# Conv stage: shifted copies by way of DRAM, the last tiles' taps behind all products, a padded sample past

## The chip, the core and the metric

One core of a Trainium2 chip runs the whole program. TensorE (PE) multiplies, VectorE (DVE), ScalarE (ACT) and GpSimd (POOL) work on rows, SyncE (SP) issues the DMAs. The metric is the device time of one execution in microseconds, the median of several runs.

## The reference

One inference step of a trunk of four layers for 512 prompt tokens and 8 sequences of 8 sample tokens, `D` = 1024, all in float32. Layers 0 and 3 have the convolution mixer that the change is about, layer 1 has attention, layer 2 pooling, and each is followed by a feed-forward block with a small convolution. The mixer:

```python
def conformer_conv(h, prefix, w_in, w_dw, ln_g, ln_b, w_out):
    a, g = jnp.split(h @ w_in, 2, axis=-1)
    u = a * jax.nn.sigmoid(g)
    up = jnp.concatenate([prefix.astype(u.dtype), u], axis=1)
    y = depthwise_causal(up, w_dw)
    y = jax.nn.silu(layer_norm(y, ln_g, ln_b))
    return y @ w_out, up[:, -(CONV_WIDTH - 1):]
```

`w_dw` has 31 taps for each of the 1024 channels. `prefix` is zero for the prompt and the last 30 rows for a sample sequence; the last 30 rows of `up` are an output.

## The kernel before

Channels lie on the partitions, tokens along the rows: 512 prompt tokens and 8 x 8 of the samples, in two halves of 288 columns. The mixer works in 8 tiles of 128 channels. For each tile i:

- **Products** (`pc`): 96 matmuls of 288 columns in tiles 2 to 7 (four groups of 24 by `mm6`), 96 by `mm3` in tiles 0 and 1, which `f_consume` runs together while the normed input comes in. A weight tile is loaded by SyncE (`raw`, 1 MB), and ScalarE and VectorE split it into two parts (`w`). The low part on VectorE frees `raw` for the next load.
- **GLU**: ScalarE's sigmoid (`sg`), then VectorE's product into `ub`, one row per channel: 30 zeros, the 512 prompt tokens, and behind them 8 sample windows of 30 past and 8 new tokens. The past comes by DMA from `sconv`.
- **Shifted copies** (`xs`, `shift` at L925): to run 31 taps as matmuls of 128 rows, 32 channels are laid out four times, each time a token further on. For each tile that is 16 copies from SBUF to SBUF of 32 rows x 540 columns (L930), eight for each half `p` of the channels.
- **Taps** (`pts`, `taps` at L938): 8 steps x 4 groups of channels, for each of which a diagonal `dg` (VectorE, `diag`) is multiplied with `xs`; a step covers four taps. They run in two visits of 4 steps each. `take` copies the result to `y` on ScalarE.
- **Sample taps** (`prods`, `tree`): products on GpSimd, sums on GpSimd or VectorE.
- `outs` (L921, L922) writes the state output `uc` in two transfers.

`f_conv_tail` then does the layer norm: a mean from tiles 0 to 5 (`st`), everything centred by it, the squares (`sq`), the exact mean and variance, and the product `pd` with `w_out` behind it (`f_out`). The taps of tile 7 run here, by halves of the tokens (256 columns).

Order: every piece is a task with an engine, a duration and a priority. `Flow.run` takes again and again the task that can start earliest, by priority among equals, so that durations and priorities set the order in which each engine's instructions are written out; on the chip each engine then runs its list in that order. `XQ` is a made-up engine that stands for the time of a transfer, `st` and `sg` count places in the shared buffers that a task takes and gives back. The products with `ada` (`adaps`), which make the scale and shift of the next normalization, are put in between.

SyncE has its own list as well: a DMA that waits holds up those behind it.

Of the kernel before, what the change touches and what calls it, by code (L numbers as in the profile page):

```python
# [30 lines left out]
D = 1024  # L31
KT = 8
NF = 22
# [6 lines left out]
XW = 512 + 4 * TG - 4  # L40

# [149 lines left out]
class Trunk:  # L191
# [681 lines left out]
    def f_conv(self, fl, l, j, dep, wdep, pdep=None):  # L873

        nc, I, O = self.nc, self.I, self.O
# [20 lines left out]
        def up(i):  # L898
            return U[i][:, 0:543]

        def us(i):
            return U[i][:, 543:847].rearrange("p (s t) -> p s t", t=38)

        def pre(i):
            U[i] = self.slot([128, 847], F32, name="ub")
            nc.gpsimd.memset(up(i)[:, 0:30], 0.0)
            nc.gpsimd.memset(up(i)[:, 542:543], 0.0)
            nc.sync.dma_start(out=us(i)[:, :, 0:30], in_=I["sconv"][j, :, i])
# [6 lines left out]
        def glu(i, h):  # L915
            pa = P[i, 0, h]
            nc.vector.tensor_tensor(up(i)[:, 30 + HP * h:30 + HP * h + HP], G[i][:, h, :HP], pa[:, :HP], OP.mult)
            nc.vector.tensor_tensor(us(i)[:, 4 * h:4 * h + 4, 30:38], self.sv(G[i][:, h]), self.sv(pa), OP.mult)

        def outs(i):  # L920
            nc.sync.dma_start(out=O["uc"][j, :, i, 0:30], in_=up(i)[:, 512:542])  # L921
            nc.sync.dma_start(out=O["uc"][j, :, i, 30:270].rearrange("p (s t) -> p s t", t=30), in_=us(i)[:, :, 8:38])  # L922
# [23 lines left out]
        def conv(i, a0, a1):  # L946
            if a0 == 0:
                P[i, "t"] = self.bank("pts")
            taps(P[i, "t"], i, a0, a1, 0, 512)

        def take(i):
            nc.scalar.activation(yv(i)[:, :, :HP], P[i, "t"].rearrange("p (a c) -> p a c", a=2), AF.Copy)

# [26 lines left out]
        val, tap_end, join_end, y = {}, {}, {}, {}  # L980
        for i in range(8):
# [24 lines left out]
            t += [fl.add("POOL", 2.7, lambda a=(i, n): prods(*a), gs, st=1, prio=pr + n) for n in range(2)]  # L1006
            fl.add("FREE", 0.0, lambda: None, t, xs, sg=1)
            t = t[1:]
            for n, d in ((16, 2.4), (8, 1.6), (4, 1.0), (2, 0.7), (1, 0.6)):
                t = fl.add(("POOL", "DVE"), (d, d / 2), lambda e, a=(i, n): tree(*a, e), t, sg=2 if n == 1 else 0,  # L1010
                           prio=pr + 2, bias=(0, 1.0))
            y[i] = [t]
            if i == 7:
                break
            t = None
            for a in range(0, TG, 4):
                t = fl.add("PE", 3.7, lambda a=(i, a, a + 4): conv(*a), t, xs, take=0 if a else 1,
                           sg=2 if a + 4 == TG else 0, prio=pr + 1)
            tap_end[i] = t
            join_end[i] = fl.add("ACT", 0.62, lambda i=i: take(i), t, give=1, prio=pr + 2)  # L1020
            y[i].append(join_end[i])
        self.w_ahead(fl, val[6][1])
        self.cv = dict(yv=yv, y=y, ready=xs, taps=taps, wdep=val[7][1], gate=[val[n][1] for n in range(8)])

    def f_conv_tail(self, fl, l, j, adep=None):

# [6 lines left out]
        q2, o, sb, sq, r, tl = {}, {}, {}, {}, {}, {}  # L1033
# [14 lines left out]
        def tap(h, a):  # L1048
            if a == 0:
                o[h] = self.bank("pts")  # L1050
            cv["taps"](o[h], 7, a, a + 4, HP * h, HP * h + HP)

        def join(h):
            nc.scalar.activation(yv(7)[:, h, :HP], o[h][:, :HP], AF.Copy)
# [51 lines left out]
        for h in range(2):  # L1106
            a = self.f_sum(fl, lambda m, h=h: yv(m)[:, h], stg[h], range(4), lambda m: True, lambda m: m in (2, 3),
                           [ready[m] for m in range(4)], take=1, prio=8000)
            a = self.f_sum(fl, lambda m, h=h: yv(m)[:, h], stg[h], range(4, 6), lambda m: False, lambda m: True, a,
                           [ready[m] for m in range(4, 6)], prio=8000)  # L1110
            a = fl.add("ACT", 0.4, lambda h=h: copy(h, 0, stg[h], "ACT"), a)
            a = self.f_mean(fl, lambda h=h: sb[h, 0], stg[h], a)
            c0.append(fl.add("ACT", 0.4, lambda h=h: nc.scalar.activation(mu(0, h), st[h][:, :H], AF.Copy, scale=8.0 / 6), a))

        last = []
        for h in range(2):
            t = None
            for a in range(0, TG, 4):
                t = fl.add("PE", 2.0, lambda h=h, a=a: tap(h, a), t, cv["ready"], take=0 if a else 1, prio=8003 + h)
            last.append(fl.add("ACT", 0.4, lambda h=h: join(h), t, give=1, prio=-1))  # L1120
        rs = []
        for h in range(2):
            cs, ss = [], []
            for m in range(8):
                if m < 6:
                    c = fl.add("POOL", 0.75, lambda h=h, m=m: centre(h, m, 0, "POOL"), c0[h], prio=8000)
                else:
                    c = fl.add("DVE", 0.36, lambda h=h, m=m: centre(h, m, 0, "DVE"), c0[h], last[h] if m == 7 else None,
                               ready[m], prio=-1)
                cs.append(c)  # L1130
                ss.append(fl.add("ACT", 0.34, lambda h=h, m=m: square(h, m), c, prio=0 if m > 5 else 8000))
                if h == 0 and m == 5:
                    fl.add("ACT", 1.5, lambda: self.table(AF.Sqrt), ss[-1], prio=0)
# [1399 lines left out]
def pack(inp, depth=DEPTH):  # L2533
# [42 lines left out]
    wd = np.concatenate([g["conv_w_dw"], np.zeros((2, 4 * TG - CW, D), f)], 1).reshape(2, TG, 4, 8, 4, 32)  # L2576
    A["wst"] = np.ascontiguousarray(wd.transpose(0, 2, 5, 3, 4, 1)).reshape(2, 128, 8, 4 * TG)

    A["sconv"] = np.ascontiguousarray(g["state_conv"].transpose(0, 3, 1, 2).reshape(2, 8, 128, 8, 30).transpose(0, 2, 1, 3, 4))
# [65 lines left out]
def out_shapes(depth=DEPTH):  # L2645
    return {
        "y": (128, 2, 8, H), "uc": (2, 128, 8, 270), "ff": (4, 128, NF, 18), "pl": (128, 8, 15), "ps": (128, 2, 32, 15),
# [17 lines left out]
def unpack(o):  # L2665
    import numpy as np
    yp, ys = unpack_x(o["y"])
    uc = o["uc"].transpose(0, 2, 1, 3).reshape(2, D, 270)
    p_conv = uc[:, :, :30].transpose(0, 2, 1)[:, None]
    s_conv = uc[:, :, 30:].reshape(2, D, 8, 30).transpose(0, 2, 3, 1)  # L2670
# [36 lines left out]
```

## Time and profile before

| | us |
|---|---|
| median of 3 runs | 2942.83 (2942.69 to 2952.84) |
| the profiled execution | 2944.08 |
| its span | 2942.3 |
| TensorE busy | 2795.8 (95%) |
| mean granted TensorE clock | 0.98 |
| conv stage of layer 0, up to the first `pd` | 58 to 274.05 |
| conv stage of layer 3, up to the first `pd` | 2213 to 2436.73 |

A profile gives, for each instruction, its start, its length, and what ended the idle time of its engine before it. A clock of 0.5 is 1.2 GHz, 1.0 is 2.4 GHz. DMA shares are of all 16 DMA engines together.

### The profile page before, as it was taken

To read this page: it belongs to the slowest core of one execution; us is meant where nothing else is said; L and a number is where in the kernel's file an instruction comes from. 1 tells how busy PE (TensorE), PEld (TensorE's weight loads), DVE (VectorE), ACT (ScalarE), POOL (GpSimd) and SP (SyncE) were. 2 spreads that over 40 slices of the span, in tenths; PEclk is the share of its full clock that TensorE was granted. 3 is DMA by queue.
4 is the path that set the end of the run, shared out by engine and by line. 5 is a ranking of instruction groups with operands and counts; after the bars stand their busy time and mean duration, and the time that the engine had idled before them with its cause. 6 is when DMAs were issued, how large, how long until landed. Compare 5 with 4: busy or idle time off the path is not lost.

```text
span 2942.3 us, 50575 instructions
## 1 busy us (share of the span) xinstructions
PE 2795.8 (95%) x20437; PEld 2473.9 (84%) x20437; DVE 1581.6 (54%) x3411; ACT 982.3 (33%) x2103; POOL 508.7 (17%) x936
## 2 busy tenths in 40 slices
PE   7898999999999999989999979999998989999998
PEld 5565799999989656889999958999997647999997
DVE  5235554454554576464455686455556336655555
ACT  3114332222355565332222244222223125422223
POOL 3234100000144234010000061000003342100001
PEclk9999999999999999999999989999999999999999
DMA  8536133334344355323322279222233453222221
GB/s 292 131 98 210 72 140 125 151 136 152 122 155 148 119 165 210 131 79 140 112 78 81 100 187 149 72 89 84 87 100 110 99 141 131 87 81 92 78 82 64
DMA packets 137705, 358.94 MB, mean 122 GB/s; under 512 B 66336, under 2 KB 72384, under 8 KB 116224
## 3 DMA queue, kind: packets, MB, share of 16 engines
q1 hardware_dynamic: 134656, 347.31, 36.8%
q0 software_dynamic: 2816, 8.39, 0.8%
q8 instruction: 162, 2.65, 0.4%
q14 instruction: 71, 0.58, 0.1%
HBM read 319.37 MB, written 18.39 MB: 115 GB/s over the span
## 4 chain that ended last, share of the span: by engine, by line
PE 79%; DMA 7%; DVE 7%; SPq 3%; issue 2%; ACT 1%; POOL 1%; DVEq 0%; ACTq 0%; POOLq 0%
PE pa L355 6%; PE pa L358 6%; PE pa L356 6%; PE pb L355 5%; PE pb L356 5%; PE pb L358 5%; PE pd L355 5%; PE pd L358 5%; PE pd L356 5%; PE pts L942 3%; PE pd L347 2%; SPq L930 2%; PE pd L348 2%; PE pd L349 2%; PE adaps L419 2%
## 5 line engine op out<-in xcount | busy, mean ns | idle before, releaser
L274 DVE TENSOR_TENSOR w<-raw,w 128x2048 fp32r<-128x2048 f32 (+1 forms) x117 | 259.4, 2217 | 388.0 <-ACT w L273 388.0
L355 PE MATMUL pa<-h,w 128*128 128x288 f32 x1280 | 363.0, 298 | 5.6 <-ACT w L273 5.6
L356 PE MATMUL pa<-h,w 128*128 128x288 f32 x1280 | 360.0, 296 | 0.0
L355 PE MATMUL pb<-h,w 128*128 128x288 f32 x1216 | 341.1, 295 | 0.0
L356 PE MATMUL pb<-h,w 128*128 128x288 f32 x1216 | 340.9, 295 | 0.0
L355 PE MATMUL pd<-u,w 128*128 128x288 f32 x1152 | 323.8, 296 | 0.0
L356 PE MATMUL pd<-u,w 128*128 128x288 f32 x1152 | 322.9, 295 | 0.0
L738 POOL COPY so<-ab 128x2 f32<-128x2 f32 x88 | 17.0, 193 | 1520.5 <-ACT ab L708 1520.5
L273 ACT ACTIVATE w<-raw 128x2048 fp32r<-128x2048 f32 (+1 forms) x117 | 218.8, 1870 | 176.2 <-PE pd L358 176.2
L358 PE MATMUL pa<-h,w 128*128 128x288 f32 x1280 | 275.2, 296 | 1.0 <-DVE w L274 1.0
L355 PEld LDWEIGHTS pa<-h,w 128*128 128x128 f32 x1280 | 242.0, 189 | 24.3 <-issue 17.6
L358 PE MATMUL pb<-h,w 128*128 128x288 f32 x1216 | 260.1, 295 | 0.0
L358 PE MATMUL pd<-u,w 128*128 128x288 f32 x1152 | 246.4, 295 | 0.0
L356 PEld LDWEIGHTS pa<-h,w 128*128 128x128 f32 x1280 | 241.9, 189 | 0.0
L355 PEld LDWEIGHTS pb<-h,w 128*128 128x128 f32 x1216 | 228.7, 188 | 0.0
L356 PEld LDWEIGHTS pb<-h,w 128*128 128x128 f32 x1216 | 228.6, 188 | 0.0
L355 PEld LDWEIGHTS pd<-u,w 128*128 128x128 f32 x1152 | 216.7, 188 | 6.7 <-issue 6.7
L303 DVE TENSOR_TENSOR w<-raw,w 128x512 fp32r<-128x512 f32 x213 | 171.5, 848 | 90.2 <-ACT w L298 89.7
L356 PEld LDWEIGHTS pd<-u,w 128*128 128x128 f32 x1152 | 216.6, 188 | 0.0
L496 DVE TENSOR_TENSOR rtmp<-pd,mod 128x32 f32<-128x32 f32 x368 | 68.6, 186 | 263.3 <-PE pd L358 174.2
L358 PEld LDWEIGHTS pa<-h,w 128*128 128x128 f32 x1280 | 206.6, 189 | 1.5 <-DVE w L274 1.5
L718 ACT ACTIVATE ab<-ab 128x576 f32<-128x576 f32 x88 | 60.4, 687 | 435.5 <-DVE ab L737 435.5
(356 smaller groups left out, 6520.5 us busy)
## 6 DMA issues: line engine op xcount, KB each, us to landing
raw<-in_w_dram SPq DMA_DIRECT2D x165, 1024.0 KB
ada<-in_ada_dram SPq DMA_DIRECT2D x192, 512.0 KB
xs<-ub SPq DMA_DIRECT2D x256, 67.5 KB
raw<-in_w_dram SPq DMA_DIRECT2D x16, 768.0 KB
x<-in_x_dram SPq DMA_DIRECT2D x8, 576.0 KB
xsp<-x SPq DMA_DIRECT2D x8, 576.0 KB
x<-xsp SPq DMA_DIRECT2D x8, 576.0 KB
out_wo_dram<-in_sw_dram SPq DMA_DIRECT2D x8, 512.0 KB
```

The lines of the kernel that those rows point to most:

```text
L273: nc.scalar.activation(w[:, 0, :width], r[:, :width], AF.Copy)
L274: self.lo_eng.tensor_tensor(w[:, 1, :width], r[:, :width], w[:, 0, :width], OP.subtract)
L303: self.eng(eng).tensor_tensor(w[:, 1, sl], r[:, sl], w[:, 0, sl], OP.subtract)
L347: nc.tensor.matmul(ps[:, :H], hi, mv(k, 0, h), start=first, stop=False)
L348: nc.tensor.matmul(ps[:, :H], hi, mv(k, 1, h), start=False, stop=False)
L349: nc.tensor.matmul(ps[:, :H], lo, mv(k, 0, h), start=False, stop=last)
L355: nc.tensor.matmul(ps[h][:, :H], hi, mv(k, 0, h), start=first, stop=False)
L356: nc.tensor.matmul(ps[h][:, :H], hi, mv(k, 1, h), start=False, stop=False)
L358: nc.tensor.matmul(ps[h][:, :H], lo, mv(k, 0, h), start=False, stop=last)
L496: nc.vector.tensor_tensor(t, self.sv(ps), self.bc(G, m, h), OP.mult)
L718: self.nc.scalar.activation(acc, acc, AF.Silu)
L942: nc.tensor.matmul(o[32 * g:32 * g + 32, :c1 - c0], DG[i][:, g * TG + a], X[i, g // 2][:, g % 2, 4 * a + c0:4 * a + c1], start=(a == 0), s ...
```

## The change

1. **Copies by way of DRAM.** `ub`'s prompt part is stored to a DRAM tensor `ub` (one transfer, 128 rows of 543), and the shifted copies are loaded from there, four transfers a tile (two for each half of the channels), each with all four shifts in the pattern of its source: 4 x 32 x 540, to 128 partitions. The zeros now are 31 in front, and the weights `wst` are padded in front instead of behind.
2. **State and past.** `sconv` comes padded to 38 columns a window, so it is one run of 304 per row; `uc` is written as one run of 334 per row, and the host takes the 30 that count.
3. **Taps.** Tiles 0 to 4: all 8 steps in one visit. Tiles 5 to 7: by halves of the tokens, behind all products (`late`), in the order 5, 6, 7 for the first half, then the second. VectorE subtracts the mean as it takes them out of PSUM (`take`, `take_s` in the tail). `diag` may run three tiles ahead.
4. **Mean.** The first mean is of tiles 0 to 3 (scale 2.0 for 8/6).
5. **Sample taps of tile 7** are on VectorE, by halves of the sequences (`prods_h`, `tree_h`).

```diff
-                for k in range(4):
-                    c = 64 * p + 32 * g
-                    nc.sync.dma_start(out=x[32 * k:32 * k + 32, g], in_=U[i][c:c + 32, k:k + XW])
+                u = I["ub"][j, i, 64 * p + 32 * g:64 * p + 32 * g + 32]
+                nc.sync.dma_start(out=x[:, g], in_=bass.AP(tensor=u.tensor, offset=u.offset, ap=[[1, 4], [UP, 32], [1, XW]]))
...
-        def conv(i, a0, a1):
-            if a0 == 0:
+        def conv(i, c0, c1):
+            if c0 == 0:
                 P[i, "t"] = self.bank("pts")
-            taps(P[i, "t"], i, a0, a1, 0, 512)
+            taps(P[i, "t"][:, c0:c1], i, 0, TG, c0, c1)
...
-            t = [fl.add("DMA", 0.7, lambda i=i: outs(i), gs, prio=pr)]
+            t = fl.add("DMA", 0.5, lambda i=i: store(i), gs, prio=pr - 1000)
+            kept = [fl.add("DMA", 0.6, lambda i=i: outs(i), gs, prio=pr), t]
+            t = fl.add("XQ", 2.5, lambda: None, t)
             xs = []
             for p in range(2):
-                x = fl.add("DMA", 2.7, lambda a=(i, p): shift(*a), gs, st=1, prio=pr - 1000)
-                xs.append(fl.add("XQ", 2.5, lambda: None, x))
-            xs.append(fl.add("DVE", 1.15, lambda i=i: diag(i), t_wr, tap_end.get(i - 2), prio=pr - 500))
...
+                x = fl.add("DMA", 1.0, lambda a=(i, p): shift(*a), t, st=1, prio=pr - 1000)
+                xs.append(fl.add("XQ", 3.5, lambda: None, x))
+            kept += xs
+            xs.append(fl.add("DVE", 1.15, lambda i=i: diag(i), t_wr, tap_end.get(i - 3), prio=pr - 500))
...
+                for h in range(2):
+                    t = fl.add("DVE", 1.15, lambda h=h: prods_h(h), gs[h], st=1, prio=-1)
+                    kept.append(t)
+                    for n, d in ((16, 0.6), (8, 0.35), (4, 0.25), (2, 0.2), (1, 0.18)):
+                        t = fl.add("DVE", d, lambda a=(h, n): tree_h(*a), t, sg=1 if n == 1 else 0, prio=-1)
+                    y[i].append(t)
...
+            if i < 5:
+                tap_end[i] = fl.add("PE", 7.3, lambda i=i: conv(i, 0, 512), xs, take=1, sg=2, prio=pr + 1)
...
+        for h in range(2):
+            for i in range(5, 8):
+                tap_end[i, h] = fl.add("PE", 3.75, lambda a=(i, HP * h, HP * h + HP): conv(*a), late[i], val[7][1],
+                                       tap_end.get((i - 1, h)), tap_end.get((i, 0)) if h else None,
+                                       take=0 if h else 1, sg=2 if h else 0, prio=7900 + 10 * h)
...
+        def take(h, m):
+
+            nc.vector.tensor_tensor(yv(m)[:, h, :HP], cv["bank"](m)[:, HP * h:HP * h + HP], mu(0, h)[:, :HP], OP.subtract)
...
+                    c = [fl.add("DVE", 0.4, lambda h=h, m=m: take(h, m), c0[h], cv["tap_end"][m, h], give=h, prio=-1),
+                         fl.add("DVE", 0.18, lambda h=h, m=m: take_s(h, m), c0[h], ready[m][h], prio=0)]
...
+    wd = np.concatenate([np.zeros((2, 4 * TG - CW, D), f), g["conv_w_dw"]], 1).reshape(2, TG, 4, 8, 4, 32)
...
+        I["ub"] = tc.nc.dram_tensor("ub", (2, 8, 128, UP), F32, kind="Internal").ap()
```

The DMA list of SyncE at tile 3 of layer 0, in the kernel before (`raw` is a weight load for a later tile, the last row belongs to tile 4):

```order
L930 DMA xs_1195<-ub_772 32x540 x8
L2491 DMA raw_1210<-in_w_dram 128x2048
L930 DMA xs_1238<-ub_772 32x540 x8
L921 DMA out_uc_dram<-ub_772 128x30
L922 DMA out_uc_dram<-ub_772 128x8x30
L930 DMA xs_1312<-ub_1072 32x540 x8
```

And in the changed kernel:

```order
L926 DMA ub<-ub_783 128x543
L923 DMA out_uc_dram<-ub_783 128x334
L2513 DMA raw_1171<-in_w_dram 128x2048
L933 DMA xs_1201<-ub 128x1x540 x2
L933 DMA xs_1204<-ub 128x1x540 x2
L926 DMA ub<-ub_1074 128x543
```

The sixteen copies with the weight load in their middle have become a store in front and four loads (two rows of two) behind the weight load.

SyncE at tile 7 of layer 0, before (`ada` are loads for the products that are put in between):

```order
L389 DMA ada_1835<-in_ada_dram 128x1024
L389 DMA ada_1837<-in_ada_dram 128x1024
L2491 DMA raw_1861<-in_w_dram 128x2048
L930 DMA xs_1873<-ub_1543 32x540 x8
L930 DMA xs_1905<-ub_1543 32x540 x8
L921 DMA out_uc_dram<-ub_1543 128x30
```

And changed, from the store of tile 7 on:

```order
L926 DMA ub<-ub_1447 128x543
L923 DMA out_uc_dram<-ub_1447 128x334
L2513 DMA raw_1835<-in_w_dram 128x2048
L391 DMA ada_1875<-in_ada_dram 128x1024
L391 DMA ada_1877<-in_ada_dram 128x1024
L933 DMA xs_1887<-ub 128x1x540 x2
L933 DMA xs_1895<-ub 128x1x540 x2
```

The loads of tile 7 now stand behind a weight load and two `ada` loads, where its copies stood behind the weight load alone.

TensorE in the tail of layer 0, before: the taps of tile 7 (`pts_1950` and `pts_1976`, one for each half of the tokens) with the sums for the layer norm between them:

```order
L942 MATMUL pts_1950<-xs_1873,dg_1665 32x256 x2
L942 MATMUL pts_1950<-xs_1905,dg_1665 32x256 x2
L540 MATMUL st_1817<-y_713,ones_85 32x288 x2
L540 MATMUL st_1817<-y_1014,ones_85 32x288 x2
L540 MATMUL sq_2027<-sq_1974,ones_85 32x288 x4
L540 MATMUL st_1770<-y_1409,ones_85 32x288 x2
L540 MATMUL st_1770<-y_1882,ones_85 32x288 x2
L540 MATMUL sq_1933<-sq_1938,ones_85 32x288 x4
L942 MATMUL pts_1976<-xs_1873,dg_1665 32x256 x2
```

And changed, where the second half of tile 7 (`pts_1976` again, by chance) begins:

```order
L945 MATMUL pts_1976<-xs_1887,dg_1445 32x256 x2
L945 MATMUL pts_1976<-xs_1895,dg_1445 32x256 x2
L421 MATMUL adaps_1933<-ada_1812,cm_92 32x512 x2
L421 MATMUL adaps_1933<-ada_1814,cm_92 32x512 x2
L542 MATMUL st_1450<-y_1353,ones_85 32x288 x2
L542 MATMUL st_1450<-y_1764,ones_85 32x288 x2
L542 MATMUL sq_1633<-sq_1617,ones_85 32x288 x4
L945 MATMUL pts_1976<-xs_1887,dg_1445 32x256 x2
```

The late taps of tiles 5 and 6 are all in front of this place now, an `ada` pair stands between the halves of tile 7, and behind its first half the sums of the first half of the tokens.

In the list of products the taps have moved back, too. Counted in single product matmuls from the first one on, those of layer 0 stand behind 246 (tile 0), 360 (2 and 1), 552 (3) and 576 (4), those of layer 3 behind 288 (0 and 1), 480 (2), 504 (3) and 624 (4), and the others behind all 768.

## Rows read from the trace of the kernel before

**Rows 1.** The page: the span, and TensorE's busy time with its share and instructions.

```profile
span 2942.3 us, 50575 instructions
...
PE 2795.8 (95%) x20437; PEld 2473.9 (84%) x20437; DVE 1581.6 (54%) x3411; ACT 982.3 (33%) x2103; POOL 508.7 (17%) x936
```

**Rows 2.** Sums by stretch: window, length, busy PE PEld DVE ACT POOL, clock, DMA share, GB/s.

```profile
58.00:274.05 216.05, 187.46 (x1416) 119.95 (x1414) 75.09 (x101) 43.60 (x91) 74.29 (x68) 0.95 0.55 150
...
2213.00:2436.73 223.73, 198.08 (x1488) 133.44 (x1486) 96.69 (x149) 53.81 (x115) 83.45 (x79) 0.95 0.48 130
```

**Rows 3.** Groups of TensorE, layer 0: busy, mean ns, idle before, what ended it.

```profile
L942 PE MATMUL pts<-xs,dg 128*32 128x512 f32 x448 | 68.9, 647 | 19.1 <-DMA xs<-ub 19.1
...
L942 PE MATMUL pts<-xs,dg 128*32 128x256 f32 x128 | 11.3, 433 | 6.4 <-DMA xs<-ub 6.4
L419 PE MATMUL adaps<-ada,cm 128*32 128x512 f32 x80 | 10.4, 597 | 0.0
```

**Rows 4.** The same view, conv stage of layer 3.

```profile
L942 PE MATMUL pts<-xs,dg 128*32 128x512 f32 x448 | 64.4, 612 | 12.2 <-DMA xs<-ub 12.0
...
L942 PE MATMUL pts<-xs,dg 128*32 128x256 f32 x128 | 10.8, 425 | 6.0 <-DMA xs<-ub 6.0
```

**Rows 5.** Sums by stretch, two of those at half clock (columns as in Rows 2).

```profile
75.20:78.60 3.40, 3.40 (x15) 0.91 (x19) 0.00 (x0) 0.00 (x0) 0.72 (x1) 0.50 0.74 101
...
2413.30:2420.10 6.80, 3.24 (x26) 1.41 (x27) 0.00 (x0) 0.00 (x0) 0.00 (x0) 0.50 0.70 158
```

**Rows 6.** Timeline of TensorE, layer 3: start, length, instruction, [idle before <-what ended it].

```profile
2277.71 0.40 PE L355 MATMUL pc<-h,w 128*128 128x288 f32 x1
...
2281.08 3.64 PE L942 MATMUL pts<-xs,dg 128*32 128x512 f32 x32
...
2295.72 4.49 PE L942 MATMUL pts<-xs,dg 128*32 128x512 f32 x28 [3.47 <-DMA xs<-ub]
...
2416.78 4.10 PE L942 MATMUL pts<-xs,dg 128*32 128x256 f32 x28 [5.47 <-DMA xs<-ub]
```

**Rows 7.** Timeline of VectorE, SyncE (SPq) and GpSimd in the same tile.

```profile
2281.99 4.48 DVE L303 TENSOR_TENSOR w<-raw,w 128x512 fp32r<-128x512 f32 x4
2282.04 5.91 SPq L930 DMA_DIRECT2D xs<-ub  x8
2282.22 2.49 POOL L961 TENSOR_TENSOR prod<-ub,par 128x960 f32<-128x960 f32 x1 [16.30 <-DVE ub L918]
...
2288.05 0.53 SPq L2491 DMA_DIRECT2D raw<-in_w_dram  x1
```

**Rows 8.** Timeline of SyncE: a weight load alone, and a store of x alone.

```profile
730.22 0.33 SPq L2491 DMA_DIRECT2D raw<-in_w_dram  x1
...
794.31 0.33 SPq L488 DMA_DIRECT2D xsp<-x  x1
```

**Rows 9.** DMA from 729.2 to 737.2, 40 slices of 0.2 us (busy tenths), packets.

```profile
DMA  4000000009903968799799595220000000000000
...
DMA packets 145, 1.07 MB, mean 133 GB/s; under 512 B 16, under 2 KB 16, under 8 KB 16
```

**Rows 10.** DMA from 794 to 799, slices of 0.125 us; queue: packets, MB, share of 16.

```profile
DMA  0000000009889998997930000000000600000000
...
q1 hardware_dynamic: 144, 0.59, 28.6%
```

**Rows 11.** DMA from 62.4 to 66.4: shifted copies alone.

```profile
DMA packets 193, 0.29 MB, mean 73 GB/s; under 512 B 64, under 2 KB 64, under 8 KB 192
...
q1 hardware_dynamic: 192, 0.28, 29.9%
```

**Rows 12.** DMA from 976.9 to 987.9: transfers of eight rows.

```profile
q1 hardware_dynamic: 224, 0.03, 1.6%
...
cvg<-cvt SPq DMA_DIRECT2D x16, 2.0 KB
```

**Rows 13.** Groups of TensorE behind the conv stage of layer 0 (columns as in Rows 3).

```profile
L419 PE MATMUL adaps<-ada,cm 128*32 128x512 f32 x52 | 8.7, 649 | 2.5 <-DMA ada<-in_ada_dram 2.5
```

More of the change, by code (lines that the diff above doesn't have):

```diff
@@ L898, in up @@
         def up(i):
-            return U[i][:, 0:543]
+            return U[i][:, 0:UP]
         def us(i):
-            return U[i][:, 543:847].rearrange("p (s t) -> p s t", t=38)
+            return U[i][:, UP:].rearrange("p (s t) -> p s t", t=38)
         def pre(i):
[L905 to L908, printed above, removed]
+            U[i] = self.slot([128, UP + 304], F32, name="ub")
+            nc.gpsimd.memset(up(i)[:, 0:31], 0.0)
+            nc.sync.dma_start(out=U[i][:, UP:], in_=I["sconv"][j, :, i])
         def sig(i, h):
@@ L916, in glu, with store @@
             pa = P[i, 0, h]
-            nc.vector.tensor_tensor(up(i)[:, 30 + HP * h:30 + HP * h + HP], G[i][:, h, :HP], pa[:, :HP], OP.mult)
+            nc.vector.tensor_tensor(up(i)[:, 31 + HP * h:31 + HP * h + HP], G[i][:, h, :HP], pa[:, :HP], OP.mult)
             nc.vector.tensor_tensor(us(i)[:, 4 * h:4 * h + 4, 30:38], self.sv(G[i][:, h]), self.sv(pa), OP.mult)
         def outs(i):
-            nc.sync.dma_start(out=O["uc"][j, :, i, 0:30], in_=up(i)[:, 512:542])
-            nc.sync.dma_start(out=O["uc"][j, :, i, 30:270].rearrange("p (s t) -> p s t", t=30), in_=us(i)[:, :, 8:38])
+            nc.sync.dma_start(out=O["uc"][j, :, i], in_=U[i][:, UP - 30:])
+        def store(i):
+            nc.sync.dma_start(out=I["ub"][j, i], in_=up(i))
         def shift(i, p):
@@ L979, in product @@
                 self.mm6([P[i, c, h] for h in range(2)], w(), k * 256 + c * 128, mv, k, k == 0, k == KT - 1)
-        val, tap_end, join_end, y = {}, {}, {}, {}
+        val, tap_end, join_end, y, late = {}, {}, {}, {}, {}
         for i in range(8):
@@ L1012, in f_conv @@
[L1012 to L1021, printed above, removed]
+                x = fl.add("DMA", 1.0, lambda a=(i, p): shift(*a), t, st=1, prio=pr - 1000)
@@ new lines, in f_conv @@
+                xs.append(fl.add("XQ", 3.5, lambda: None, x))
+            kept += xs
+            xs.append(fl.add("DVE", 1.15, lambda i=i: diag(i), t_wr, tap_end.get(i - 3), prio=pr - 500))
+            if i < 7:
+                t = [fl.add("POOL", 2.7, lambda a=(i, n): prods(*a), gs, st=1, prio=pr + n) for n in range(2)]
+                kept += t
+                for n, d in ((16, 2.4), (8, 1.6), (4, 1.0), (2, 0.7), (1, 0.6)):
+                    t = fl.add(("POOL", "DVE"), (d, d / 2), lambda e, a=(i, n): tree(*a, e), t, sg=2 if n == 1 else 0,
+                               prio=pr + 2, bias=(0, 1.0))
+                y[i] = [t, t]
+            else:
+                y[i] = []
+                for h in range(2):
[4 more added lines that the diff above has]
+                    y[i].append(t)
@@ new lines, in f_conv @@
+            fl.add("FREE", 0.0, lambda: None, kept, sg=1)
+            if i < 5:
+                tap_end[i] = fl.add("PE", 7.3, lambda i=i: conv(i, 0, 512), xs, take=1, sg=2, prio=pr + 1)
+                join_end[i] = fl.add("ACT", 0.62, lambda i=i: take(i), tap_end[i], give=1, prio=pr + 2)
+                y[i].append(join_end[i])
+            else:
+                late[i] = xs
+        for h in range(2):
[3 more added lines that the diff above has]
+                                       take=0 if h else 1, sg=2 if h else 0, prio=7900 + 10 * h)
@@ L1022, in f_conv @@
         self.w_ahead(fl, val[6][1])
-        self.cv = dict(yv=yv, y=y, ready=xs, taps=taps, wdep=val[7][1], gate=[val[n][1] for n in range(8)])
+        self.cv = dict(yv=yv, y=y, bank=lambda i: P[i, "t"], tap_end=tap_end, wdep=val[7][1], gate=[val[n][1] for n in range(8)])
     def f_conv_tail(self, fl, l, j, adep=None):
@@ L1106, in f_conv_tail @@
         for h in range(2):
[L1107 to L1110, printed above, removed]
+            a = self.f_sum(fl, lambda m, h=h: yv(m)[:, h], stg[h], range(4), lambda m: True, lambda m: True,
+                           [ready[m] for m in range(4)], take=1, prio=6000)
             a = fl.add("ACT", 0.4, lambda h=h: copy(h, 0, stg[h], "ACT"), a)
             a = self.f_mean(fl, lambda h=h: sb[h, 0], stg[h], a)
[L1113 to L1120, printed above, removed]
+            c0.append(fl.add("ACT", 0.4, lambda h=h: nc.scalar.activation(mu(0, h), st[h][:, :H], AF.Copy, scale=2.0), a))
         rs = []
```

48 lines of the change are left out of this document (25 added, 23 removed).

## The prediction

> **What bounds the kernel now.** I read the page first: TensorE is busy 95% of the span [rows 1], so a stage is worth what TensorE waits in it. Then the sums by stretch for the two conv stages, each up to the first matmul into `pd`: in layer 0 TensorE is busy 187.5 of 216.05 us at a mean clock of 0.95, in layer 3 198.1 of 223.7 [rows 2]: 28.6 and 25.6 us idle. The groups of instructions say what ended the idle time: before the taps it is always the shifted copies, 19.1 + 6.4 us in layer 0 and 12.0 + 6.0 in layer 3 [rows 3, 4], together 43.5 us. Third, the granted clock: eight stretches of 3.4 us (two of them 6.8) run at 0.50, 34 us in all, half of it lost, 17 us [rows 5] (two of the eight). So all that the change can win in the conv stages is about 60 us.
>
> Why the copies are late is seen in one tile of layer 3. Its last group of 24 products runs from 2277.71 to 2281.08 (3.37 us, so 13.5 for a tile), and a half of the taps takes 3.64, a whole 7.28 [rows 6]. The GLU ends at 2282.0. SyncE then issues eight copies (5.91 us), the weight load `raw` at 2288.05, and eight more; the last taps get their copy at 2295.72, 14.6 us after the product ended [rows 6, 7]. Issue time and the weight load in the middle make up that delay.
>
> **The change, part by part.** *Issues.* Sixteen copies of 0.7 to 0.8 us each go; a store, one state output in place of two, and four loads come. SyncE gets some 8 us a tile back, off the path: what counts is when the last load lands.
>
> *Where the loads stand.* In the new order each tile's row is store, output, `raw`, four loads. `raw` waits, as before, for VectorE to finish the low halves of the weights, at 2281.99 + 4.48 = 2286.47, 5.4 us after the product ended [rows 7], and the loads stand behind it. A `raw` alone, issued at 730.22 [rows 8], has its last packets in slice 27 of 0.2 us from 729.2, 4.4 us after issue [rows 9]. So a tile's loads begin 5.4 + 4.4 = 9.8 us after its product. The store is hidden under this: one of 576 KB, issued at 794.31 [rows 8], had its last data packets in slice 21 of 0.125 us from 794, 2.3 us after issue [rows 10], and the new one is of 271 KB, and the GLU before it 1 us.
>
> *How long the loads take.* This the trace of before doesn't show. A load has 128 rows of 2160 bytes, but its source is written as 4 shifts by 32 rows by 540, its destination as 128 partitions. The nearest rows: the copies of 32 rows leave 192 packets for four, 64 of them small: 32 rows and 16 small ones each [rows 11]. The `raw` leaves 128 + 16 [rows 9]. The transfers of eight rows leave 224 for fourteen that landed, all small: 16 each, so eight rows and eight others [rows 12]. I read the extra packets as one completion for each engine used: sixteen, but eight where there are only eight rows. So a transfer seems to be dealt out by its outermost dimension. With four there I take it that the load runs on four engines; were it dealt by the 128 partitions, it would be sixteen. The Trainium skill, page "DMA: Bandwidth & Descriptors", section "Why a DMA increments its semaphore by 16 and not by 1", says the same more sharply: the number of engines is the largest up to 16 that divides the slowest dimension of both sides, which here is four. By that page the four are always the lowest-numbered; no row here shows which they are.
>
> In the sum all loads queue on the same four engines. Were each dealt to a different four, a tile's loads would take as long as on sixteen.
>
> A packet: the 4608-byte rows of the store take 28.6% of 16 engines in 5 us, 22.9 us for 128, 179 ns [rows 10], which by bytes is 84 ns for 2160. The copies of 2160 bytes now take 29.9% of 16 x 4 us, 19.1 us for 128, 149 ns [rows 11]; those are short transfers from SBUF to SBUF, 2 rows an engine. The loads stream, as the store does, so I take 86 ns. Four engines: 32 packets a load, 128 a tile, 11 us (19 at the other end). Sixteen engines: 2.8 us (4.8).
>
> So, after its product, a tile's copies are there at 9.8 + 11 = 21 us on four engines, or, when the engines still have the tile before, 14 us after that one (its `raw` share, 3 us, and 11). On sixteen it is 12.6 us.
>
> *New places of the taps.* The change moves them back, whole tiles at a time, and those of tiles 5 to 7 behind all products. I put the waits together from the order, with 3.37 for 24 products, 7.28 for a tile's taps, 1.04 for an `ada` pair (10.4 us for ten [rows 3]). Layer 3, time 0 at the end of products(1), on four engines: copies(0) at -3.4 + 21 = 17.6, wanted at 13.5: wait 4.1, taps end 24.9. Copies(1) at 31.4: wait 6.5, end 38.7. Products of 2 and 3, interleaved, end at 48.8 and 52.2; copies(2) at 69.8, wanted at 65.7: 4.1. Copies(3) at 83.8, wanted at 80.5: 3.3. Taps(4): products(4) end at 94.5, copies at 115.5, wanted at 109: 6.5. Products 6 and 7 end at 131 and 144.5. Tile 5 waits nothing; tile 6 has its copies at 152, wanted at 149.2: 2.8; tile 7, behind 6 on the same engines, at 166, wanted at 164: 2. Sum 29. Layer 0 in the same way: 4.8 (0), 5.1 (2), 9.2 (1), 4.2 (3), 3.3 (4), 2.6 (6) and 4.4 (7, whose loads stand behind a `raw` that waits for GpSimd and two `ada` loads): 34. Together 63 us of waits in place of 43.5: +19.5. On sixteen engines none of these is left.
>
> *Other edits.* Moving the `ada` loads ahead takes away the 2.5 us wait of layer 0 and the 1.0 of layer 3 [rows 13] (the second is of the same kind): -3.5. The clock: fourteen waits of 2 to 9 us replace some 25 of 0.3 to 5.5 [rows 6] (the longest, and one of the middle); I take the same loss, 17 us, bounds -9 and +9. Whole visits of the taps, rather than halves, spare a few switches: -2, bounds -8 and 0. The tail changes work at equal cost: VectorE centres tiles 5 to 7 straight from PSUM instead of ScalarE copying first, and it does the sample taps of tile 7 under the late taps; if that cover fails, two half tiles of them stand before the last sums; GpSimd now takes 2.5 us for one half of a tile's products [rows 7], so bound +5. The mean over four tiles needs no sums of tiles 4 and 5 and is early. Wider `sconv` and `uc` rows: one run a partition for eight, off the path.
>
> Sum against the profiled 2944.08 us (0.04% over the median 2942.83): +19.5 - 3.5 + 0 - 2 = +14, less 2 for the median and rounding: **2956 us**.
>
> **Rivals.** *Sixteen engines.* For it: all transfers with 128 partitions in this trace leave 16 small packets. Against: none of them has a first dimension of four on one side. Then 43.5 of copies, 3.5 of `ada`, 15 of the 17 of the clock and 2 to 5 of switches go: -64 to -67, and in the tail, at full clock, a few more: 2876 us (2862 to 2892).
>
> *Four engines and slow packets*, the one on the other side: if a packet on the four engines costs the 149 ns of the present copies, a tile's loads take 19 us, and with its `raw` 22 us, more than the 20.8 of a tile's products and taps: then the copies set the pace, at some 8 us more in nine of the fourteen waits, +72: 3028. It decides from about 130 ns a packet. Against it: the store's rate.
>
> *Half effect*: the loads use eight engines or overlap from two ends: 5.5 us a tile, copies at 15.3, nearly all hidden: some 2895.
>
> That the order is not what it says is no rival: the order of the built kernel has the taps where I count them.
>
> **How the numbers follow.** Four engines at the store's rate 0.52, own range 2925 to 2985 (the waits can be wrong by 15, the clock by 9, the tail by 5); sixteen engines 0.36; eight 0.05; slow packets 0.07. The range takes the first two: 2862 to 2985, leaving out the slow packets and the edges. About 0.5% (15 us) is what a measurement can tell, so the bounds lie at 2928 and 2957.5. Faster: 0.35 of the sixteen, 0.05 of the eight, 0.03 of the four: 0.43. Within: 0.26 of the four and 0.01: 0.27. Slower: 0.23 of the four and 0.07: 0.30. The forecast itself stands just under the upper bound.
>
> **What would show it.** The packets of a load: 128 + 4 if four engines, 128 + 16 if sixteen. The stretch of a tile's loads: DMA share at a quarter for 11 us, or full for 3. Taps with one wait a tile of 3 to 9 us, or none. `raw` to the next products: no new wait on `w`. If the idle time before the taps falls under 10 us in both layers and the time doesn't reach 2900, the clock or the tail has taken it, and my sum is wrong there. If the waits are there but under 40 us together, the start of the loads (9.8 us) is what I have too late.

## The result: slower by 1.45%, on the side of the four engines

The changed kernel takes 2988.28 us (median of 4 runs, 2984.4 to 2990.8), the kernel before 2942.76: a ratio of 1.0145, interval 1.012 to 1.017. That is 3 us over the upper end of the range. The profiled execution has a span of 2982.6 us against 2942.3 [rows 1], 40.3 more.

The two conv stages first, as sums by stretch (window, length, busy time of PE, PEld, DVE, ACT, POOL, then clock, DMA share, GB/s), up to the first `pd`; these answer to [rows 2]:

```profile
58.00:303.78 245.78, 204.04 (x1578) 124.79 (x1576) 79.99 (x113) 41.52 (x88) 70.60 (x63) 0.88 0.51 161
2228.36:2477.90 249.54, 204.66 (x1632) 141.82 (x1631) 107.61 (x162) 53.79 (x115) 78.67 (x68) 0.89 0.44 141
```

Layer 0 is 29.7 us longer than the 216.05 of before, layer 3 25.7 longer than 223.83 (counted, as here, from its first product at 2212.90): 55.4 together. 15 us come back elsewhere, 8 of them behind the stage of layer 0, where 16 `ada` matmuls are left in place of 52 [rows 13]. TensorE was idle for 54 us in the two stages and is for 87 now, and the mean clock has gone from 0.95 and 0.95 to 0.88 and 0.89.

The groups of TensorE in the same two stretches, first layer 0, then layer 3 (busy, mean ns | idle before, and what ended it); they answer to [rows 3, 4]:

```profile
L945 PE MATMUL pts<-xs,dg 128*32 128x512 f32 x320 | 60.0, 740 | 25.9 <-DMA xs<-ub 25.9
L945 PE MATMUL pts<-xs,dg 128*32 128x256 f32 x384 | 30.0, 437 | 12.6 <-DMA xs<-ub 12.6
L421 PE MATMUL adaps<-ada,cm 128*32 128x512 f32 x112 | 15.5, 598 | 0.0
...
L945 PE MATMUL pts<-xs,dg 128*32 128x512 f32 x320 | 53.2, 679 | 17.6 <-DMA xs<-ub 17.6
L945 PE MATMUL pts<-xs,dg 128*32 128x256 f32 x384 | 26.6, 407 | 7.4 <-DMA xs<-ub 7.4
L421 PE MATMUL adaps<-ada,cm 128*32 128x512 f32 x56 | 9.8, 655 | 11.0 <-DMA ada<-in_ada_dram 11.0
```

The `ada` products of layer 3 before:

```profile
L419 PE MATMUL adaps<-ada,cm 128*32 128x512 f32 x32 | 5.5, 594 | 1.0 <-DMA ada<-in_ada_dram 1.0
```

The copies are still what TensorE waits for, 63.5 us in place of 43.5, and in layer 3 the `ada` loads have become late, 11.0 us in place of 1.0.

What a wait looks like now is seen in the timeline of TensorE at the taps of tile 0 of layer 0:

```profile
77.45 1.04 PE L945 MATMUL pts<-xs,dg 128*32 128x512 f32 x2
79.75 1.05 PE L945 MATMUL pts<-xs,dg 128*32 128x512 f32 x2 [1.26 <-DMA xs<-ub]
82.48 1.04 PE L945 MATMUL pts<-xs,dg 128*32 128x512 f32 x2 [1.69 <-DMA xs<-ub]
85.26 9.70 PE L945 MATMUL pts<-xs,dg 128*32 128x512 f32 x58 [1.73 <-DMA xs<-ub]
```

A tap step needs one matmul pair from each of the four channel groups, and each group has its own load. The loads come 2.7 to 2.8 us apart here, and each lets two matmuls go. Four loads one behind the other, each of 32 packets to an engine at 86 ns, would be 2.75 us apart. The remaining 58 matmuls then take 9.70 us; at full clock they took 58/64 of 7.28, 6.6.

That the loads run on four engines is seen in the DMA view from 226.7 to 232.3, where two loads of tile 5 land (a row of 40 slices of 0.14 us in tenths of 16 engines; packets; the queue's packets, MB and share):

```profile
DMA  2222222222227222232132232222322221321322
...
DMA packets 270, 0.58 MB, mean 104 GB/s; under 512 B 8, under 2 KB 8, under 8 KB 269
...
q1 hardware_dynamic: 269, 0.56, 25.9%
```

A quarter of the 16 engines is busy, all the time, and two loads leave eight small packets, four each, where a copy from SBUF left sixteen [rows 11]. That is what the prediction asked for as a sign.

### The profile page after: what moved, and what is told of

Its sections match the earlier page's. It is cut to its first block, busy times and chain, and to the rows that moved or that the text cites. A ratio compares the mean times of both kernels' runs of the same rounds, so it can differ in the third digit from the quotient of the medians.

```text
span 2982.6 us, 50711 instructions
## 1 busy us (share of the span) xinstructions
PE 2803.2 (94%) x20677; PEld 2479.5 (83%) x20677; DVE 1600.6 (54%) x3432; ACT 975.2 (33%) x2090; POOL 510.9 (17%) x922
## 4 chain that ended last, share of the span: by engine, by line
PE 80%; DMA 9%; DVE 6%; issue 1%; SPq 1%; ACT 1%; POOL 1%; DVEq 0%; POOLq 0%; ACTq 0%
PE pa L357 6%; PE pa L360 6%; PE pa L358 6%; PE pb L357 5%; PE pb L358 5%; PE pb L360 5%; PE pd L357 5%; PE pd L358 5%; PE pd L360 5%; DMA xs<-ub 5%; PE pd L349 2%; PE pts L945 2%; PE pd L350 2%; PE pd L351 2%; PE adaps L421 2%
## 5 line engine op out<-in xcount | busy, mean ns | idle before, releaser
L945 PE MATMUL pts<-xs,dg 128*32 128x256 f32 (+1 forms) x1408 | 169.8, 553 | 63.5 <-DMA xs<-ub 63.5
L305 DVE TENSOR_TENSOR w<-raw,w 128x512 fp32r<-128x512 f32 x201 | 163.2, 853 | 96.2 <-ACT w L300 95.6
```

The source lines that it names most:

```text
L305: self.eng(eng).tensor_tensor(w[:, 1, sl], r[:, sl], w[:, 0, sl], OP.subtract)
L945: nc.tensor.matmul(o[32 * g:32 * g + 32, :c1 - c0], DG[i][:, g * TG + a], X[i, g // 2][:, g % 2, 4 * a + c0:4 * a + c1], start=(a == 0), s ...
```

## The experiments

Each was run with the kernel before beside it, on the same chip; a ratio is to that one. The kernels are named by where the taps stand (old or late) and by what carries the copies (4 or 16 engines, or SBUF).

**The same loads on sixteen engines.** The source with the 32 channels outermost, and the rows of the weights and of the diagonal's mask in that order:

```diff
-    ap=[[1, 4], [UP, 32], [1, XW]]
+    ap=[[UP, 32], [1, 4], [1, XW]]
-    wd.transpose(0, 2, 5, 3, 4, 1)
+    wd.transpose(0, 5, 2, 3, 4, 1)
-    (p % 32)[:, None] == np.arange(32)[None, :]
+    (p // 4)[:, None] == np.arange(32)[None, :]
```

> The changed kernel, but each load's source is written with the 32 channels outermost and the four shifts inside (32 x 4 x 540 instead of 4 x 32 x 540), with the rows of the weights and of the diagonal's mask in the same order; nothing else moves. Theory A (a transfer is dealt out by its outermost dimension, so the loads ran on four engines): the idle time before the taps falls from 63.5 us to under 10, the mean clock of the two conv stages rises from 0.88 and 0.89 to 0.95 or more, and the time falls by 80 to 120 us, to 2870 to 2910. Rival B (the way through DRAM, store, wait and load behind the weight load, is what costs): idle time before the taps stays over 45 us, time over 2965.

Measured: 2865.83 us, ratio 0.970 (0.968 to 0.972), and again:

> The changed kernel with the loads on sixteen engines, once more, beside the others of this call. 2.7 to 3.3% under before.

2864.29, ratio 0.970 (0.969 to 0.972). So the order of one access pattern is worth some 4% of the kernel (0.970 against 1.0145), and turns the change from a loss of 1.4% into a gain of 3.0%. The loads of a tile in its DMA view, from 178.7 to 181.6, slices of 0.07 us (the first of their packets lie before it):

```profile
DMA  9999979999999999998999999999893000000000
...
DMA packets 467, 0.88 MB, mean 305 GB/s; under 512 B 64, under 2 KB 64, under 8 KB 466
```

All engines are at work, and four transfers leave 64 small packets. The sums by stretch and the taps of layer 0:

```profile
58.00:233.41 175.41, 172.20 (x1573) 121.58 (x1571) 79.24 (x112) 41.54 (x88) 70.79 (x63) 1.00 0.61 223
2167.08:2361.77 194.69, 183.84 (x1632) 139.26 (x1630) 109.30 (x162) 53.80 (x115) 79.42 (x68) 0.97 0.50 179
...
L945 PE MATMUL pts<-xs,dg 128*32 128x512 f32 x320 | 38.6, 594 | 0.5 <-DMA xs<-ub 0.5
```

The waits before the taps are gone (0.5 us), the clock is at 1.00 and 0.97, the stages are 70 and 55 us shorter. Theory A holds, with a time 4 us under the range that I gave, and rival B falls: with the store, the wait for it and the weight load in front all in the same places of the same list, nothing is late.

**The order alone**, which here means the late places together with the new tail. The changed kernel with the sixteen copies from SBUF of before:

```diff
-                u = I["ub"][j, i, 64 * p + 32 * g:64 * p + 32 * g + 32]
-                nc.sync.dma_start(out=x[:, g], in_=bass.AP(...))
+                for k in range(4):
+                    nc.sync.dma_start(out=x[32 * k:32 * k + 32, g], in_=U[i][c:c + 32, k:k + XW])
```

> The changed kernel with the sixteen copies from SBUF of before in place of the store and the four loads; the order of all other work as changed. Theory A: the later places of the taps alone are good, as they give the copies time: the waits before the taps are under 30 us, time 2890 to 2930. Rival C (the later, whole visits of the taps and their tail are what costs): time over 2960, with waits on the copies no longer the largest.

2925.88, ratio 0.990 (0.988 to 0.992). The waits on the copies are 27.6 us (18.6 and 8.9), as theory A had it, and the later places are no loss: rival C falls.

**The way through DRAM alone**, in the kernel before, taps in two visits and its own tail, first on sixteen engines, then on four:

```diff
+            s = fl.add("DMA", 0.5, lambda i=i: store(i), gs, prio=pr - 1000)
+            s = fl.add("XQ", 2.5, lambda: None, s)
...
-                x = fl.add("DMA", 2.7, lambda a=(i, p): shift(*a), gs, st=1, prio=pr - 1000)
-                xs.append(fl.add("XQ", 2.5, lambda: None, x))
+                x = fl.add("DMA", 1.0, lambda a=(i, p): shift(*a), s, st=1, prio=pr - 1000)
+                xs.append(fl.add("XQ", 3.5, lambda: None, x))
```

> The kernel before with the way through DRAM alone (store, and four loads dealt by 32 channels), taps in two visits of four steps each as the planner places them with the changed costs of the transfers, the tail as before. Theory A: the copies are there 12 to 15 us after a tile's product instead of 14 to 16, and the planner places the taps later: idle before the taps 10 to 25 us, time 2900 to 2930. Rival B: as before or slower, 2940 to 2970.

2908.95, ratio 0.985 (0.983 to 0.987), waits on the copies 11.6 us.

> The kernel before with the way through DRAM alone, four loads dealt by the four shifts as in the changed kernel (four engines), the taps in two visits as the planner places them, the tail as before. Theory A: each tile's loads take 11 us on four engines, as there; the taps are placed earlier than in the changed kernel, so that the waits are longer: idle before the taps 70 to 110 us, time 3.5 to 6% over its sister on sixteen engines, 1.5 to 4.5% over before. Rival C (the late places are what costs): not slower than before by more than 1%.

3013.24, ratio 1.022 (1.019 to 1.025), 3.8% over its sister. The waits on the copies are 68 us by the groups (34.9 + 9.4 and 23.8), a little under what I expected, and the `ada` loads are waited for 16.2 us in layer 3. The table, as ratios to the kernel before:

| taps | copies from SBUF | DRAM, 16 engines | DRAM, 4 engines |
|---|---|---|---|
| two visits, old tail | 1 | 0.985 | 1.022 |
| late places, new tail | 0.990 | 0.970 | 1.014 |

On sixteen engines both parts of the change pay, and together they give 0.970, a little more than 0.985 x 0.990, which is 0.975. The upper row is not at one set of places: told the new costs, the planner put the visits of layer 0 24 to 48 products later in both DRAM kernels than in the kernel before, so 0.985 holds the way and these places together. The two DRAM kernels of a row do have the same order, and there the four engines cost 3.8% in the upper row and 4.5% in the lower.

**The changed kernel once more, and its trickle.** First unaltered, as a base for its variants:

> The changed kernel itself, unaltered, beside the others of this call on the same chip. Both theories: slower than before by 1.2 to 1.7%, waits before the taps 60 to 67 us, clock of the conv stages 0.87 to 0.90.

2988.14, ratio 1.014 (1.011 to 1.017). Then with the groups of a tap step in the order 3 to 0:

```diff
-                for g in range(4):
+                for g in range(3, -1, -1):
```

> The changed kernel with the four channel groups of a tap step in the order 3, 2, 1, 0 instead of 0 to 3, so that TensorE waits first for the load that lands last and then runs all taps at once, where it now does two matmuls for each load that lands. Theory D (the trickle of two matmuls a load holds the clock down on top of the waits): the idle time stays at 60 to 75 us, now in one piece a tile, and the half-clock time of the two stages, 113 us in the profile of the changed kernel, moves by over 15 us, the kernel's time with half of that; I expect it to fall, to 90, time lower by 8 to 14 us. Rival F (the copies' arrival alone sets the pace, whatever TensorE does in between): the time stays within 5 us of the changed kernel.

2992.43, ratio 1.016 (1.013 to 1.018): no difference to the base that these runs can tell. The sums by stretch of layer 0, first the base, then this run, the place of tile 0 in the timeline, and the groups of the taps in the two layers:

```profile
58.00:306.40 248.40, 203.44 (x1577) 124.76 (x1575) 79.96 (x113) 41.52 (x88) 70.65 (x63) 0.88 0.50 160
58.00:305.30 247.30, 185.44 (x1568) 124.86 (x1567) 79.20 (x112) 41.51 (x88) 70.58 (x63) 0.86 0.50 159
...
84.56 9.27 PE L945 MATMUL pts<-xs,dg 128*32 128x512 f32 x64 [8.14 <-DMA xs<-ub]
...
L945 PE MATMUL pts<-xs,dg 128*32 128x512 f32 x320 | 45.2, 729 | 41.8 <-DMA xs<-ub 41.8
L945 PE MATMUL pts<-xs,dg 128*32 128x256 f32 x384 | 25.7, 427 | 16.3 <-DMA xs<-ub 12.6 <-DVE prod L969 3.7
...
L945 PE MATMUL pts<-xs,dg 128*32 128x512 f32 x320 | 40.3, 661 | 30.2 <-DMA xs<-ub 30.2
L945 PE MATMUL pts<-xs,dg 128*32 128x256 f32 x384 | 26.5, 424 | 6.7 <-DMA xs<-ub 6.7
```

The stage has the length of its base (248.4), but the wait is one piece, 8.1 us for tile 0. My theory D on the trickle falls: the clock is not better for it (0.86; 0.88 in the base), the time at half clock in the two stages rose from 106 to 126 us, and the kernel's time did not follow. Rival F holds, 4.3 us from the base. And the run shows how much is waited for in truth: 41.8 + 12.6 us in layer 0 and 30.2 + 6.7 in layer 3, 91.3 us, where the groups of the base show 42 and 25. The difference was counted as busy: a pair alone between two waits counts 1.04 us, where a pair in a run of 64 takes 0.23 (7.28 us for the run), and TensorE's busy time in layer 0 falls from 203.4 to 185.4 us at the same length of the stage.

**Work in the waits.** The changed kernel with 32 products ahead of the visits that wait:

```diff
+            if i < 5 or (i > 5 and c0 == 0):
+                for n in range(32):
+                    nc.tensor.matmul(P[i, "t"][:, :H], hh[0, 0, 0][:, 0, :128], hh[0, 0, 0][:, 1], start=True, stop=True)
             taps(P[i, "t"][:, c0:c1], i, 0, TG, c0, c1)
```

> The changed kernel with 32 products of 288 columns, whose results are overwritten, ahead of the taps of tiles 0 to 4 and of the first half of tiles 6 and 7 (14 places, 4.4 us each at full clock, 62 us of added work): they keep TensorE at work while the copies are on their way. Theory D (some 34 of the 45 us lost are the clock, which falls where TensorE gets only two matmuls for each load that lands): clock of the conv stages up to 0.95, idle before the taps from 63.5 to under 30 us, time 2955 to 2975 in spite of the added work. Rival E (the clock follows from something else): clock stays under 0.91, time 2985 to 3020.

2982.66, ratio 1.010 (1.008 to 1.012). Its stages, tile 0 again (the first row are the added products), the groups of the taps in layer 0, and of the taps and the `ada` products in layer 3:

```profile
58.00:303.02 245.02, 219.86 (x1784) 150.30 (x1782) 78.42 (x109) 41.53 (x88) 70.82 (x63) 0.94 0.51 158
2228.95:2478.60 249.65, 223.21 (x1857) 166.89 (x1855) 107.76 (x162) 53.75 (x115) 78.91 (x68) 0.94 0.43 141
...
75.04 4.42 PE L954 MATMUL pts<-h 128*128 128x288 f32 x32
79.39 2.19 PE L945 MATMUL pts<-xs,dg 128*32 128x512 f32 x6
83.32 7.05 PE L945 MATMUL pts<-xs,dg 128*32 128x512 f32 x58 [1.74 <-DMA xs<-ub]
...
L945 PE MATMUL pts<-xs,dg 128*32 128x512 f32 x320 | 49.6, 645 | 13.1 <-DMA xs<-ub 13.1
L945 PE MATMUL pts<-xs,dg 128*32 128x256 f32 x384 | 28.1, 418 | 7.9 <-DMA xs<-ub 7.9
...
L945 PE MATMUL pts<-xs,dg 128*32 128x512 f32 x320 | 44.2, 623 | 6.5 <-DMA xs<-ub 6.5
L421 PE MATMUL adaps<-ada,cm 128*32 128x512 f32 x56 | 9.0, 660 | 11.1 <-DMA ada<-in_ada_dram 11.1
```

The clock is up to 0.94 in both stages and the waits on the copies are down from 63.5 to 27.5 us (13.1 + 7.9 and 6.5), as theory D has it, yet the stages are as long as before and the time missed its 2955 to 2975. 62 us of added work took the place of 36 us of waits, and of time at half clock and in single pairs. At tile 0 the gain is plain: with 4.42 us of work added the 58 matmuls end at 90.37 instead of 94.96. Of these 4.6 us, 2.7 are the clock's, as the matmuls take 7.05 us instead of 9.70; the rest is that the last load lands sooner in this run. So the clock does cost time there. At the end of the stage a load is waited for all the same: in layer 0 the copies of tiles 6 and 7 (7.9 us), in layer 3 the `ada` loads (11.1 us, as in the changed kernel).

**The stores.** In the changed kernel a tile's loads wait for its store, and the store was issued behind the loads of the tile before, which hold the four engines. SyncE at tile 7 of layer 0 in the changed kernel:

```profile
249.48 0.33 SPq L926 DMA_DIRECT2D ub<-ub  x1
250.24 0.34 SPq L923 DMA_DIRECT2D out_uc_dram<-ub  x1
256.74 0.33 SPq L2513 DMA_DIRECT2D raw<-in_w_dram  x1
259.40 1.48 SPq L391 DMA_DIRECT2D ada<-in_ada_dram  x2
265.13 4.75 SPq L933 DMA_DIRECT2D xs<-ub  x4
```

```diff
-            nc.sync.dma_start(out=I["ub"][j, i], in_=up(i))
+            nc.scalar.dma_start(out=I["ub"][j, i], in_=up(i))
```

> The changed kernel (four engines) with the store of each tile issued by ScalarE's queue in place of SyncE's. Theory G (the stores stand in the same four engines' queues behind the loads of the tile before: tile 7's store in layer 0 is issued at 249.5 and its loads at 265.1): the loads of tile 7 begin 4 to 10 us earlier, waits before the taps fall by 8 to 20 us, time 10 to 20 us under the changed kernel. Rival: the store lands as late, since the engines are the same: within 5 us.

2992.90, ratio 1.014 (1.012 to 1.015): theory G falls on the time, which stays within the rival's 5 us. Tile 7's loads on SyncE in this run, then the last wait of TensorE for them, in the changed kernel and in this run:

```profile
260.75 7.25 SPq L933 DMA_DIRECT2D xs<-ub  x4
...
284.85 5.26 PE L945 MATMUL pts<-xs,dg 128*32 128x256 f32 x57 [2.98 <-DMA xs<-ub]
...
283.11 5.65 PE L945 MATMUL pts<-xs,dg 128*32 128x256 f32 x57 [2.81 <-DMA xs<-ub]
```

The loads are issued at 260.75, 4.4 us earlier, but the last of them is there only 1.7 us earlier, and the waits on the copies hardly move (26.6 + 13.7 and 17.4 + 6.1, 63.8). The rival's reason is not what happened: by the semaphore records of the traces tile 7's store landed 9.0 us after its issue in place of 15.6. So the store's place is not what makes the loads late. What is left is the four engines' own work; no run here takes that apart.

**Round the better version.** Three changes of the one on sixteen engines. The planner told that two loads take 1.2 us:

```diff
-                xs.append(fl.add("XQ", 3.5, lambda: None, x))
+                xs.append(fl.add("XQ", 1.2, lambda: None, x))
```

> The changed kernel with loads on sixteen engines (32 channels outermost) and the planner told so: 1.2 us for the transfer of two loads instead of 3.5. The taps move some 4 us earlier in the list. Theory A: the copies are there 12.6 us after a tile's product, against the planner's 8 or so, so some waits come back: 5 to 15 us, time 0 to 12 us over the one with 3.5. Rival: the earlier taps free the buffers sooner and it is faster by 3 to 8 us.

2905.95, ratio 0.986 (0.984 to 0.988): 41 us slower, over three times what I had as the upper end. The waits on the copies are 19.3 us (5.8 + 6.0 and 5.9 + 1.6), and 8.7 us on `ada` loads come on top, with the clock at 0.96. With 4.5 us instead:

> The same with 4.5 us instead of 3.5 in the planner for the transfer of two loads, so that the taps come later still. The waits before the taps are 0.5 us with 3.5 already, so nothing is left to win there: time within 8 us of it, if the longer hold of the buffers costs nothing; over 10 us more if it does.

2878.47, ratio 0.976 (0.974 to 0.977), 14 us slower: no wait on the copies at all, but 11.6 us on `ada` loads in layer 3:

```profile
L421 PE MATMUL adaps<-ada,cm 128*32 128x512 f32 x64 | 16.4, 718 | 11.6 <-DMA ada<-in_ada_dram 11.6
```

And with tiles 5 and 6 among the products:

```diff
-            if i < 5:
+            if i < 7:
-            for i in range(5, 8):
+            for i in range(7, 8):
```

> The same (sixteen engines, 3.5) with tiles 5 and 6 taken in whole visits among the products, and tile 7 alone behind them by halves. Theory: keeping three tiles back gives the copies of tile 7 time and TensorE work under the layer norm: without it the wait before tile 7 comes back, 5 to 10 us a layer, 10 to 20 us in all. Rival: the late tiles only move work: within 6 us.

2896.59, ratio 0.982 (0.980 to 0.983), 32 us slower, more than I expected. The late tiles do pay. The groups of layer 0:

```profile
L945 PE MATMUL pts<-xs,dg 128*32 128x512 f32 x448 | 55.7, 594 | 1.2 <-ACT sg L915 0.9 <-DMA xs<-ub 0.2
L421 PE MATMUL adaps<-ada,cm 128*32 128x512 f32 x128 | 23.9, 686 | 10.8 <-DMA ada<-in_ada_dram 10.7
```

The groups show hardly a wait on the copies; it is the `ada` loads that are waited for, 10.7 us here and 8.0 in layer 3. That does not settle my reason: the `ada` products stand in front of the taps of tile 7 in this list, and by the trace's semaphore records tile 7's copies landed at 231.4 to 233.6, between the two waits for `ada` that end at 228.7 and 234.9. Without these products TensorE would have had to wait for the copies. So the version on sixteen engines with the planner's 3.5 is the best here, 3.0% under the kernel before.

## Why the prediction was off

It named the mechanism and took the right case: four engines, 2.75 us a load, the waits moved and not removed. It was wrong in the sizes of three terms, and the time fell 3 us outside its range. The step that failed most is the clock's, "I take the same loss": the loss grew by some 16 us where the sum had 0. The next is that the `ada` loads would no longer be waited for: in layer 3 they cost 11.0 us.

*How the loads are dealt:* right, by the small packets, by the quarter share and by the experiment that undoes it. The reading of the eight-row transfers [rows 12] was enough for it: four small packets a load in the changed kernel, sixteen in the other order. The rule in the Trainium skill, page "DMA: Bandwidth & Descriptors", section "Why a DMA increments its semaphore by 16 and not by 1", gives four for this pattern and sixteen for the other order, and both traces agree with it. 86 ns a packet was right too where the loads run alone (269 packets in 25.9% of 16 engines in 5.6 us).

*The rival of sixteen engines* was given 2876 (2862 to 2892); it was measured at 2866 and 2864, beside a kernel before that took 2954 and 2949 there. By the ratio of 0.970 that is 2855 on the 2943 of the prediction, 7 us under its range.

*The waits, +19.5:* the groups show 63.5 us, and I had 63. But that agreement is luck. My chain put one wait before each visit, and counted in one piece they are 91. The 43.5 that I set it against is a count in pieces too. The waits of the weight loads (PEld) hold most of the time of the single pairs; for the copies they are, in the kernel before and in the changed one (us, times):

```profile
  PEld pts L942: 64.1, 32
  PEld pts L945: 91.2, 31
```

That is +27, by the groups +20. The difference came out near, since both of its sides were too small. The chain was short because copies came later than it had them. Tile 2 of layer 0 shows one reason. SyncE there:

```profile
100.02 0.33 SPq L926 DMA_DIRECT2D ub<-ub  x1
...
102.87 0.33 SPq L926 DMA_DIRECT2D ub<-ub  x1
108.83 0.33 SPq L2513 DMA_DIRECT2D raw<-in_w_dram  x1
...
110.79 2.76 SPq L933 DMA_DIRECT2D xs<-ub  x4
```

`raw` is issued 8.8 us after the store that follows the GLU, not 4.4, because the store of tile 1 and another wait for VectorE stand before it in this order. The start of a tile's loads, 9.8 us after its product, was read from one tile of layer 3 and carried to all.

Tile 7 shows two more reasons. Its store, which I had hidden with 2.3 us, landed 15.6 us after its issue in layer 0, and the loads were issued when it had (265.13). And the loads come 4.1 us apart there, not 2.75:

```profile
276.68 0.62 PE L945 MATMUL pts<-xs,dg 128*32 128x256 f32 x2 [1.72 <-DMA xs<-ub]
280.81 1.06 PE L945 MATMUL pts<-xs,dg 128*32 128x256 f32 x2 [3.51 <-DMA xs<-ub]
```

The third is the line at 284.85 above. That is 128 ns a packet, close to the 130 from which the rival of slow packets was to decide. The weight load and the `ada` loads issued from 256.74 on lie next to them; that these slow the loads is likely, but no run takes them away.

*The `ada` loads, -3.5:* the 2.5 us behind the stage of layer 0 are gone, as I had it, but in layer 3 the sign is wrong, 11.0 us of waits in place of 1.0. They stand on SyncE's list behind the loads, and I put their own queue on the four engines into the sum of layer 0 only as a delay of the copies, not as a thing that TensorE waits for.

*The clock, 0 within 9:* the largest miss. Its mean fell by 0.07 and 0.06. Summed over the records where a stretch at half clock and a busy TensorE overlap, it is 32.6 us before and 75.4 after; half of that would be 16 and 38, +21. This is an upper estimate, since a pair at half clock between two waits holds nothing up. Counted only where matmuls follow one another without a wait, against their mean distance at full clock, the half clock cost 14 us before and 30 after in the same traces: +16, beyond my bound of 9. I reasoned from the number of waits, fourteen for some twenty-five. The waits are longer now, and so are the stretches at half clock: in [rows 5] they last 3.4 or 6.8 us; now they reach 13.7. That the one follows from the other is my reading; no run parts them. My count of eight stretches before had also left out one of 6.8 us in layer 3 (2215.3 to 2222.1), which changes the loss before little.

Idle time +32 and busy time +23 make the 55 of the stages; less 15 elsewhere, the 40 of the span. Of the busy time 16 are the clock's, and some 7 are 56 `ada` matmuls more that now lie in the stages (168 for 112 by the groups, 0.13 us each at full clock [rows 3]); most of these are then missing behind layer 0, among the 15 us that I didn't count. Of the 26 by which my +14 fell short, the clock's 16 and the 11 of the `ada` loads of layer 3 are about all; what else was off is smaller or cancels. How much shorter the kernel would be at full clock with the same waits stays open: the added products raise the clock only by work of their own, and what they won was waited for again at the end of the stages.

*The tail:* that the change is of equal cost there held but for one thing: `pd` now waits 4.3 us for VectorE in either layer, where it was 0.8 us. The timeline of the changed kernel:

```profile
303.77 0.40 PE L349 MATMUL pd<-h,w 128*128 128x288 f32 x1 [1.15 <-ACT h L1131]
308.50 0.61 PE L350 MATMUL pd<-h,w 128*128 128x288 f32 x1 [4.32 <-DVE h L1133]
```

The version on sixteen engines has the same 4.3 us in both layers. Why was not looked into; there is something left to win.

## What to carry to other kernels

Before a transfer is merged from several, look at the outermost dimension of both its sides: a pattern whose first count is four put a load on four of the sixteen engines, and here the order of two dimensions was worth 4%. The small packets in the profile, counted for each transfer, told how many engines it had: four here, sixteen in the other order. When a wait is split into pieces by transfers that land one behind the other, the idle time in the groups understates it (67 us against 91 here); a variant that waits for the last one first shows its true length. And a planner's cost for a transfer is also a distance: told the shorter time that the transfer itself takes, it put the taps ahead of the copies, which still stood behind a weight load, and gave back half of the gain.

## What was not expected of the hardware

Transfers on all engines are held up by those on four. By the semaphore records of the traces, in layer 0 the store of tile 7, issued behind the loads of tile 6, landed 15.6 us after its issue in the changed kernel, and 7.5 us in the version on sixteen engines, at the same place of the same list; a store with no loads in front took 2.5 us. In layer 3 the waits on `ada` loads are 11.0 us against none on sixteen engines. And ScalarE's own queue gave little: issued there, the store landed after 9.0 us and the loads were issued 4.4 us earlier, but the waits stayed at 64 us.
